# A two-layer decoder trunk on one core: half of the attention's key blocks on GpSimd in place of a third, roots by way of PSUM, head norms ahead in the queues

## The chip, the core and the metric

One core of a Trainium2 chip runs the whole program. The metric is device time in microseconds, the median of three runs. TensorE is PE here, VectorE DVE, ScalarE ACT, GpSimd POOL, and SyncE, which issues the DMAs, SP.

## What is computed

Two layers over 2048 positions of width 1024, in float32. Layer 0 is gated linear attention (GLA), layer 1 forgetting attention (FoX) with 16 heads of 64. After each mixer a per-layer embedding is added (PLE: a projection times the sigmoid of a gate). A norm ends it. The part that the change touches most:

```python
def fox_mixer(h, w_in, b_f, q_gain, k_gain, w_out):
    q, k, v, g, f_logit = jnp.split(h @ w_in, ...)
    log_f = jax.nn.log_sigmoid(f_logit + b_f)
    qh = rms_norm(to_heads(q, FOX_HEADS), q_gain)   # the head norms
    kh = rms_norm(to_heads(k, FOX_HEADS), k_gain)
    o = fox_attention(qh, kh, vh, log_f)            # softmax(q k^T / 8 + c[t] - c[s], causal) v
    return (o * jax.nn.silu(g)) @ w_out
```

## The kernel before

Positions are cut into four chunks of 512 columns (c = 0 to 3); a tile is 128 partitions by 512 columns, one PSUM bank. Every float32 operand of a large matmul is split into a high part, rounded to the matmul's type, and a low part, the rest; a product is three matmuls (high by high, high by low, low by high). Names end in h and l for the parts: xnh, xnl the normed input, ogh, ogl the gated mixer output, wh, wl weights, kh, kl temporaries.

Streams (Python generators: dense work, attention, maxima, norms, gates) emit operations to a planner, `Streams` (L72), which simulates the engines with its own costs and decides the order of every engine; the program is then written in that order and each engine runs its queue strictly in it. Operations that are ready on an engine go by level and then by age (`able`, L206 to L210); a lower level goes first. All instructions bear the line of the planner's call, so they are told apart by tile names.

In layer 1, `attention` (L1331) takes heads in order. For a head and chunk it goes over nk = 4(c+1) key blocks of 128 keys. For a block PE computes the scores pS (As with B, Es with Dc) into a PSUM bank; ACT makes exp into Ph (rounded) and a second, full exp; the difference is Pl; PE adds V by Ph and V by Pl to the output po two blocks later (LAG). Blocks whose number is a multiple of G_OF put the full exp into SBUF (P0, accg or Pf: names P, ag, Pf in the trace) and let POOL take the difference and the running sum accg (ag). The other blocks put it back into the bank and let DVE take the difference (Pl<-bank) and the sum (acc<-bank). At the end of a head POOL adds accg to acc. `maxima` (L1269) computes the scores' maxima one head ahead: a matmul (Dm with Es) per 128 queries into a bank, a DVE maximum (mx), and at the end of the head m4c, a transpose on PE and a row of Es. At most M_LIVE of these matmuls are under way.

`qk_unit` (L1212) projects a pair of heads and norms them: a square on ACT, high part kh on ACT and low part kl on POOL, a sum over the head by a matmul with onesb, `rsqrt` (L620), y, and the parts again. `rsqrt` is Ln, Exp and Square on ACT and two DVE instructions: q = (pin + eps) q, and out = (q - 1.5) y, both into SBUF (names rs). `join` (L1414) does the denominators of a head pair in the same manner.

`out1` (L1500) is the output projection of a chunk, `ple1` (L1507) its PLE, `finish` (L1492) the last norm: eight instructions hr<-hr,gcol,rs on DVE, each followed by a store. A chunk's attention output that comes before the PLE of the chunk ahead is stored in DRAM (os) and reloaded by way of hx, in two buffers, when that PLE is done.

Of the kernel before, what the change touches and what calls it, by code (L numbers as in the profile page):

```python
# [16 lines left out]
ALU = mybir.AluOpType  # L17
# [9 lines left out]
EPS = 1e-6  # L27
GH, DK, DV = 4, 128, 256
FH, HD = 16, 64
# [4 lines left out]
PARTS = ("xnh", "xnl", "ogh", "ogl", "hr")  # L34


BANKS, K_D, K_V, K_M, M_LIVE = 8, 0, 0, 1, 3

PB, PF, PL, LAG = 3, 2, 3, 2

# [9 lines left out]

V_KS, N_O, N_G = ((0,), (1,), (2, 3), (4, 5), (6, 7)), 5, 2

G_OF = 3

Q_W, Q_C, Q_M = -1, 1, 1
P_A, P_M, P_D = 2.5, 0.5, 3

POOL_F = 3
# [13 lines left out]
class Streams:  # L72
# [19 lines left out]
    def spawn(self, gen, prio):  # L92
        self.count += 1
        self.streams.append([prio, self.count, gen, self.now])

    def mark(self, key):
        self.marks[key] = self.now
# [109 lines left out]
    def at(self, *aps):  # L207

        return self.over([self.hist[k][0] for x in aps for k in self.parts(x) if k in self.hist and self.hist[k][0]])
# [38 lines left out]
    def bank(self, keep=0):  # L248

        return lambda: sorted(self.over(q)() for q, i in self.banks)[keep] if len(self.banks) > keep else INF  # L250
# [6 lines left out]
    def give(self, ap):  # L257
        self.banks.append((self.users(ap), self.bankno[ap.tensor.name]))
# [53 lines left out]
def trunk_kernel(ctx: ExitStack, tc: tile.TileContext, a: dict, out: bass.AP, layers: int = 2):  # L312
# [4 lines left out]
    nc = SimpleNamespace(vector=Engine(nc0.vector, sq_, "V"), scalar=Engine(nc0.scalar, sq_, "A"), gpsimd=Engine(nc0.gpsimd, sq_, "G"), sync=Engine(nc0.sync, sq_, "H"))  # L317
# [29 lines left out]
    @contextmanager  # L347
    def level(n):

        sq_.level += n  # L350
        try:
            yield
        finally:
            sq_.level -= n
# [4 lines left out]
    def psa(name):  # L359
        return banks[sq_.take()]  # L360
# [4 lines left out]
    def parted(src, square, eng):  # L365

        hl = [tmp.tile([P, T], F32R, tag="k" + x, name="k" + x, bufs=KB) for x in "hl"]
        if square:
            q = t2("q", "sq", 2)
            nc.scalar.activation(q, src, AF.Square)  # L370
            src = q
        split(*hl, src, eng)
        return hl

    def total(name, w, src, square, eng):

        yield tmp.able("kh", KB)
        hl = parted(src, square, eng)
        names = {x.tensor.name for x in hl}
        tmp.held |= names  # L380
        yield at(*hl)
        yield bank()
        pn = psa(name)
        for n in range(2):
            mm(pn, w, hl[n], start=(n == 0), stop=(n == 1))
        tmp.held -= names
        return pn

    def t2(name, tag, bufs):
        return tmp.tile([P, T], F32, tag=tag, name=name, bufs=bufs)  # L390

    def mm(dst, w, x, start=True, stop=True):
        n = dst.free_size()
        sq_.op("P", [dst], [w, x], max(n, 64) * (4 if x.dtype == F32 or n < 256 else 1) / 2400.0 + 0.0134, partial(nc0.tensor.matmul, dst, w, x, start=start, stop=stop))
# [4 lines left out]
    def rdma(dst, src):  # L399
        nc.sync.dma_start(dst.bitcast(F32), src.bitcast(F32))  # L400


    def split(hi, lo, src, eng):
        nc.scalar.copy(hi, src)
        eng.tensor_tensor(lo, src, hi.bitcast(F32), ALU.subtract)
# [172 lines left out]
    def steps(pairs, dst, n0, total):  # L578

        for n, (w, x) in enumerate(pairs):  # L580
            yield at(w, x)
            mm(dst, w, x, start=(n0 + n == 0), stop=(n0 + n == total - 1))
# [8 lines left out]
    def unit(name, x, nm):  # L591

        yield bank(K_D)
        dst = psa(name)
        for i in range(2):
            yield from half(dst, x, nm, i)
        return dst
# [22 lines left out]
    def rsqrt(pin, scale, out=None):  # L620
        yq = tmp.tile([P, 2, T], F32, tag="rs", name="rs", bufs=2)
        n = pin.free_size()
        y, q = yq[:, 0, 0:n], yq[:, 1, 0:n]
        nc.scalar.activation(y, pin, AF.Ln, bias=epsb, scale=scale)
        nc.scalar.activation(y, y, AF.Exp, scale=-0.5)
        nc.scalar.activation(q, y, AF.Square, scale=(0.5 * scale) ** 0.5)
        nc.vector.scalar_tensor_tensor(q, pin, EPS / scale, q, ALU.add, ALU.mult)
        q2 = q if out is None else out
        nc.vector.scalar_tensor_tensor(q2, q, 1.5, y, ALU.subtract, ALU.mult)
        return q2  # L630

    def sigmoid(z, tag, bufs):
# [8 lines left out]
    class SumSq:  # L641
# [36 lines left out]
        def root(self, out=None):  # L678
            pn = yield from total("nq_p", onesr, self.acc, False, nc.vector)
            r = rsqrt(pn, 1.0 / D, out)  # L680
            give(pn)
            return r
# [177 lines left out]
    L = {}  # L860
# [351 lines left out]
    def qk_unit(c, u, col):  # L1212

        pq = yield from unit("pqk", xn, "wqk")

        def rest():
            if col == 0 or u:

                yield ("sum", c, 2 * u - col)
            pn = yield from total("qk_n", L["onesb"], pq, True, nc.gpsimd)  # L1220
            mark(("sum", c, 2 * u + 1 - col))
            yield tmp.able("kh", KB)
            r = rsqrt(pn, 1.0 / HD)
            give(pn)
            y = t2("qk_y", "ny", 2)
            nc.vector.scalar_tensor_tensor(y, pq, L["qkg"][:, col : col + 1], r, ALU.mult, ALU.mult)
            give(pq)
            nm = "qk"[col]
            hi = tmp.tile([P, T], F32R, tag="kh", name=nm + "h", bufs=KB)
            lo = tmp.tile([P, T], F32R, tag="kl", name=nm + "l", bufs=KB)  # L1230
            split(hi, lo, y, nc.gpsimd)
            for j in range(2):
                js = slice(j * HD, (j + 1) * HD)
                d = L["KS"][c][2 * u + j] if col else L["QS"][2 * u + j][c]
                rdma(d[64:128], (hi if col else lo)[js])
                rdma(d[0:64], (lo if col else hi)[js])
            mark(("qk"[col], c, u))

        spawn(rest(), 0)
# [91 lines left out]
    def attention():  # L1331
        nxt = None
        for i in range(NCH * FH):
# [11 lines left out]
            for kb in range(nk):  # L1345
# [21 lines left out]

                if kb % G_OF == 0:
                    if kb == 0:
                        Pf = P0 = L["f"].tile([P, T], F32, tag="P0", name="P0", bufs=2)  # L1370
                    elif kb == G_OF:
                        Pf = accg = L["f"].tile([P, T], F32, tag="ag", name="ag", bufs=2)
# [6 lines left out]
                    nc.gpsimd.tensor_tensor(Pl[:, c0:], Pf[:, c0:], Ph[:, c0:].bitcast(F32), ALU.subtract)  # L1379
                    if kb > G_OF:  # L1380
                        with level(Q_C):
# [32 lines left out]
    def join(c, h, po, acc):  # L1414

        i, u = h % 2, h // 2
        if i == 0:
            pair["o"] = L["f"].tile([P, T], F32, tag="op", name="op", bufs=1)
        op = pair["o"]
        own, oth = slice(i * 64, i * 64 + 64), slice(64 - i * 64, 128 - i * 64)  # L1420
        hb = t2("hb", "sq", 2)
        nc.scalar.copy(hb[own], po[oth])
        nc.vector.tensor_tensor(op[own], hb[own], po[own], ALU.add)
        give(po)
        pair[i] = acc
        if i == 0:
            return
        a0, a1 = pair[0], pair[1]

        def rest():  # L1430
            yield at(a0, a1)
            yield ("sg1", c, u)
            yield bank()
            pd = psa("den")
            mm(pd, L["onesh"][:, 0], a0, stop=False)
            mm(pd, L["onesh"][:, 1], a1, start=False)
            yq = tmp.tile([P, 2, T], F32, tag="rs", name="dn", bufs=2)
            y, q = yq[:, 0], yq[:, 1]
            nc.scalar.activation(y, pd, AF.Ln)
            nc.scalar.activation(y, y, AF.Exp, scale=-1.0)  # L1440
            nc.vector.tensor_tensor(q, pd, y, ALU.mult)
            give(pd)
            nc.vector.scalar_tensor_tensor(q, q, 2.0, y, ALU.subtract, ALU.mult)
            nc.vector.scalar_tensor_tensor(q, op, -1.0, q, ALU.mult, ALU.mult)
            nc.gpsimd.tensor_tensor(q, q, sgs[c, u], ALU.mult)
            if c and ("ple1", c - 1) not in sq_.marks:

                nc.sync.dma_start(os[c][:, u], q)
                later.append((c, u))
            else:  # L1450
                split(og[0][:, u], og[1][:, u], q, nc.gpsimd)
            mark(("den", c, u))
            mark(("og1", c, u))

        spawn(rest(), 0)

    sgs, later = {}, []
# [153 lines left out]
```

## Time and profile before

| what | value |
|---|---|
| median of three runs | 3096.41 us (3092.79 to 3096.66) |
| the profiled execution | 3096.0 us, its span 3094.3 us |
| PE, busy share | 97% |
| DVE, ACT, POOL, busy share | 72%, 62%, 37% |
| granted TensorE clock, mean | 0.987 |
| on the chain that ended last | PE 86%, DVE 6%, DMA 3%, ACT 2% |

Layer 0 takes about the first 1100 us. A busy PE counts also matmuls at half clock, so the number of matmuls in a stretch says more than the share. An engine's idle time is put down to what ended it.

### The profile page before, as it was taken

To read this page: it belongs to the slowest core of one execution; us is meant where nothing else is said; L and a number is where in the kernel's file an instruction comes from. 1 tells how busy PE (TensorE), PEld (TensorE's weight loads), DVE (VectorE), ACT (ScalarE), POOL (GpSimd) and SP (SyncE) were. 2 spreads that over 40 slices of the span, in tenths; PEclk is the share of its full clock that TensorE was granted. 3 is DMA by queue.
4 is the path that set the end of the run, shared out by engine and by line. 5 is a ranking of instruction groups with operands and counts; after the bars stand their busy time and mean duration, and the time that the engine had idled before them with its cause. 6 is when DMAs were issued, how large, how long until landed. Compare 5 with 4: busy or idle time off the path is not lost.

```text
span 3094.3 us, 43470 instructions
## 1 busy us (share of the span) xinstructions
PE 3000.7 (97%) x13568; PEld 2418.8 (78%) x13568; DVE 2225.9 (72%) x3979; ACT 1905.0 (62%) x3651; POOL 1136.0 (37%) x941
## 2 busy tenths in 40 slices
PE   8989999999999999999999999999999999999887
PEld 6878887888788878777788776888777878778666
DVE  7686767667765765675766768775888788888835
ACT  6565665657565465664656656565757677667635
POOL 1232222213222234453433424343545455455531
PEclk9999999999999999999999999999999999999989
DMA  5565667556632567987768776778677677666654
GB/s 192 183 209 177 204 201 234 187 195 214 218 109 82 178 189 246 279 266 249 228 215 273 234 224 204 228 213 263 215 241 228 216 243 227 208 190 193 209 175 140
DMA packets 379737, 648.15 MB, mean 209 GB/s; under 512 B 43097, under 2 KB 78433, under 8 KB 379506
## 3 DMA queue, kind: packets, MB, share of 16 engines
q1 hardware_dynamic: 379506, 645.37, 65.6%
q8 instruction: 108, 1.77, 0.2%
q14 instruction: 123, 1.01, 0.1%
HBM read 521.86 MB, written 123.21 MB: 208 GB/s over the span
## 4 chain that ended last, share of the span: by engine, by line
PE 86%; DVE 6%; DMA 3%; ACT 2%; issue 1%; POOL 1%; SPq 1%; DVEq 0%; ACTq 0%; POOLq 0%
PE bank L176 86%; DVE ny L176 1%; DMA B<-KS 1%; DVE rs L176 1%; DMA Dm<-KS 1%; DVE mx L176 1%; DMA hx<-hs 1%; SPq L176 1%; ACT rs L176 1%; DVE hr L176 1%; DVE Pl L176 0%; DVE acc L176 0%; ACT Ph L176 0%; DVE wl L176 0%; DVE ogl L176 0%
## 5 line engine op out<-in xcount | busy, mean ns | idle before, releaser
L176 ACT ACTIVATE Ph<-bank 128x512 fp32r<-128x512 f32 (+2 forms) x640 | 335.9, 545 | 95.1 <-PE bank L176 45.1
L176 DVE TENSOR_TENSOR wl<-wr,wh 128x512 fp32r<-128x512 f32 x332 | 264.6, 804 | 158.2 <-ACT wh L176 126.9
L176 PE MATMUL bank<-xnh,wh 128*128 128x512 f32 x1128 | 323.8, 397 | 0.8 <-ACT Ph L176 0.6
L176 PE MATMUL bank<-xnl,wh 128*128 128x512 f32 x1128 | 322.6, 394 | 0.0
L176 PE MATMUL bank<-xnh,wl 128*128 128x512 f32 x1128 | 322.3, 393 | 0.0
L176 DVE TENSOR_TENSOR Pl<-bank,Ph 128x512 fp32r<-128x512 f32 (+2 forms) x400 | 245.9, 615 | 74.0 <-ACT bank L176 72.3
L176 DVE TENSOR_REDUCE mx<-bank 128x1 f32<-128x512 f32 x384 | 249.2, 682 | 54.9 <-PE bank L176 53.8
L176 PE MATMUL bank<-ogh,wh 128*128 128x512 f32 x912 | 260.6, 397 | 15.9 <-ACT ogh L176 15.9
L176 ACT CAST wh<-wr 128x512 fp32r<-128x512 f32 x332 | 203.0, 615 | 113.7 <-PE bank L176 57.5
L176 PE MATMUL bank<-ogl,wh 128*128 128x512 f32 x912 | 258.4, 395 | 1.0 <-DVE ogl L176 0.9
L176 PE MATMUL bank<-ogh,wl 128*128 128x512 f32 x912 | 255.8, 393 | 0.0
L176 PE MATMUL bank<-As,B 128*128 128x512 f32 (+2 forms) x640 | 242.6, 379 | 7.2 <-DMA B<-KS 3.2
L176 PEld LDWEIGHTS bank<-xnh,wh 128*128 128x128 f32 x1128 | 211.2, 189 | 47.7 <-ACT Ph L176 1.5
L176 PE MATMUL bank<-Pl,V 128*128 128x512 f32 (+2 forms) x640 | 238.3, 372 | 9.6 <-POOL Pl L176 5.8
L176 PEld LDWEIGHTS bank<-xnl,wh 128*128 128x128 f32 x1128 | 210.2, 189 | 42.7 <-issue 0.2
L176 PEld LDWEIGHTS bank<-xnh,wl 128*128 128x128 f32 x1128 | 209.5, 188 | 42.8 <-issue 0.6
L176 PE MATMUL bank<-Ph,V 128*128 128x512 f32 (+2 forms) x640 | 238.4, 372 | 0.1
L176 PE MATMUL bank<-Es,Dc 128*128 128x512 f32 (+2 forms) x640 | 236.4, 369 | 1.6 <-DMA Es<-mr 1.6
L176 PE MATMUL bank<-Dm,Es 128*128 128x512 f32 (+2 forms) x640 | 223.4, 376 | 10.8 <-DVE acc L176 7.6
L176 ACT ACTIVATE bank<-bank 128x512 f32<-128x512 f32 (+2 forms) x400 | 219.2, 548 | 0.0
L176 PEld LDWEIGHTS bank<-ogh,wh 128*128 128x128 f32 x912 | 171.7, 190 | 54.5 <-ACT ogh L176 19.1
L176 POOL TENSOR_TENSOR ag<-ag,Pf 128x512 f32<-128x512 f32 (+1 forms) x112 | 125.2, 1118 | 211.9 <-ACT Pf L176 172.1
(271 smaller groups left out, 7077.2 us busy)
## 6 DMA issues: line engine op xcount, KB each, us to landing
B<-KS SPq DMA_DIRECT2D x160, 256.0 KB
V<-VS SPq DMA_DIRECT2D x160, 256.0 KB
Dm<-KS SPq DMA_DIRECT2D x160, 132.0 KB
Dc<-KS SPq DMA_DIRECT2D x160, 132.0 KB
wr<-gla_wv SPq DMA_DIRECT2D x64, 256.0 KB
wr<-gla_wqk SPq DMA_DIRECT2D x64, 256.0 KB
wr<-gla_wg SPq DMA_DIRECT2D x64, 256.0 KB
wr<-gla_wo SPq DMA_DIRECT2D x64, 256.0 KB
```

The source lines that it names most:

```text
L176: q.emit()
```

## The change

Five constants and places change. G_OF goes from 3 to 2, so POOL takes every second key block. M_LIVE goes from 3 to 2. The first DVE instruction of `rsqrt` and of the denominators writes its result into the PSUM bank that it reads, and the second reads it there, so that neither reads two SBUF tensors. A level Q_N = -1 is put on the square, parts, root and y of the head norms.

```diff
-BANKS, K_D, K_V, K_M, M_LIVE = 8, 0, 0, 1, 3
+BANKS, K_D, K_V, K_M, M_LIVE = 8, 0, 0, 1, 2
...
-G_OF = 3
+G_OF = 2
...
+Q_N = -1
...
-    def total(name, w, src, square, eng):
+    def total(name, w, src, square, eng, lv=0):
 
         yield tmp.able("kh", KB)
-        hl = parted(src, square, eng)
+        with level(lv):
+            hl = parted(src, square, eng)
...
         nc.scalar.activation(q, y, AF.Square, scale=(0.5 * scale) ** 0.5)
-        nc.vector.scalar_tensor_tensor(q, pin, EPS / scale, q, ALU.add, ALU.mult)
+
+        nc.vector.scalar_tensor_tensor(pin, pin, EPS / scale, q, ALU.add, ALU.mult)
         q2 = q if out is None else out
-        nc.vector.scalar_tensor_tensor(q2, q, 1.5, y, ALU.subtract, ALU.mult)
+        nc.vector.scalar_tensor_tensor(q2, pin, 1.5, y, ALU.subtract, ALU.mult)
...
-            pn = yield from total("qk_n", L["onesb"], pq, True, nc.gpsimd)
+            pn = yield from total("qk_n", L["onesb"], pq, True, nc.gpsimd, Q_N)
             mark(("sum", c, 2 * u + 1 - col))
             yield tmp.able("kh", KB)
-            r = rsqrt(pn, 1.0 / HD)
+            with level(Q_N):
+                r = rsqrt(pn, 1.0 / HD)
+                y = t2("qk_y", "ny", 2)
+                nc.vector.scalar_tensor_tensor(y, pq, L["qkg"][:, col : col + 1], r, ALU.mult, ALU.mult)
             give(pn)
-            y = t2("qk_y", "ny", 2)
-            nc.vector.scalar_tensor_tensor(y, pq, L["qkg"][:, col : col + 1], r, ALU.mult, ALU.mult)
             give(pq)
...
-            nc.vector.tensor_tensor(q, pd, y, ALU.mult)
+            nc.vector.tensor_tensor(pd, pd, y, ALU.mult)
+            nc.vector.scalar_tensor_tensor(q, pd, 2.0, y, ALU.subtract, ALU.mult)
             give(pd)
-            nc.vector.scalar_tensor_tensor(q, q, 2.0, y, ALU.subtract, ALU.mult)
```

The planner then orders every engine anew. Each engine's instructions are the same in number but for those named in the prediction; three places are shown.

DVE at the end of attention, before: the last norm of chunk 2 (hr), with the blocks of the head before the last (Pl, acc) and the maxima of the last head (mx, printed as ISA) around it.

```order
L176 SCALAR_TENSOR_TENSOR rs_192<-rs_192 128x512
L176 TENSOR_TENSOR Pl_8138<-bank_90,Ph_8137 128x384
L176 SCALAR_TENSOR_TENSOR hr<-hr,gcol,rs_192 128x512 x8
L176 TENSOR_TENSOR acc_8153<-bank_90,acc_8153 128x384
L176 TENSOR_TENSOR bank_92<-bank_92,limT 128x128
```

And now, the same eight instructions; op is the output of the last head pair, kl the split of the norm's sum.

```order
L178 TENSOR_TENSOR op_8150<-sq_184,bank_93 64x512
L178 SCALAR_TENSOR_TENSOR ny_166<-bank_89,ny_166 128x512
L178 TENSOR_TENSOR ny_166<-ny_166,bank_88 128x512
L178 TENSOR_TENSOR nacc_235<-nacc_235,sq_185 128x512
L178 TENSOR_TENSOR kl_201<-nacc_235,kh_200 128x512
...
L178 SCALAR_TENSOR_TENSOR bank_90<-bank_90,rs_162 128x512
L178 SCALAR_TENSOR_TENSOR rs_162<-bank_90,rs_162 128x512
L178 SCALAR_TENSOR_TENSOR hr<-hr,gcol,rs_162 128x512 x8
L178 TENSOR_TENSOR pl_228<-rs_192,ph_227 128x512 x2
```

Before, an acc and all that follows of the last head come behind the eight; now the last head's last op comes ahead of them.

PE in the last head, before, from the transpose of its maxima (ident) on:

```order
L176 MATMUL bank_92<-ident,m4c_8155 4x128
L176 MATMUL bank_93<-As_8043,B_8134 128x512
L176 MATMUL bank_93<-Es_8046,Dc_8051 128x512
L176 MATMUL bank_87<-Ph_8140,V_8152 128x256
L176 MATMUL bank_87<-Pl_8141,V_8152 128x256
L176 MATMUL bank_89<-As_8043,B_8134 128x512
L176 MATMUL bank_89<-Es_8046,Dc_8051 128x512
L176 MATMUL bank_87<-Ph_8142,V_8152 128x256
L176 MATMUL bank_87<-Pl_8143,V_8152 128x256
```

And now, a few blocks into the last head:

```order
L178 MATMUL bank_89<-As_8043,B_8134 128x512
L178 MATMUL bank_89<-Es_8046,Dc_8051 128x512
L178 MATMUL bank_87<-ogh,wh_102 128x512 x2
L178 MATMUL bank_87<-ogl,wh_102 128x512 x4
L178 MATMUL bank_87<-ogh,wl_103 128x512 x3
L178 MATMUL bank_93<-Ph_8137,V_8135 128x512
L178 MATMUL bank_93<-Pl_8138,V_8135 128x512
L178 MATMUL bank_90<-As_8043,B_8134 128x512
L178 MATMUL bank_90<-Es_8046,Dc_8051 128x512
```

Before, scores and values follow each other with nothing between; now matmuls of ple1(2) (ogh, ogl) stand between the blocks.

PE between the last of ple1(2) (ph, pl by weights) and out1(3) (ogh by wh_96) in the new order; xnh, xnl is the last gate, onesh a denominator, onesr the sum of the norm.

```order
L178 MATMUL bank_88<-ph_227,wl_101 128x512 x2
L178 MATMUL bank_92<-xnh,wh_102 128x512 x4
...
L178 MATMUL bank_92<-xnh,wxl_8035 128x512 x4
L178 MATMUL bank_91<-acc_8153,onesh 128x512
L178 MATMUL bank_91<-acc_8136,onesh 128x512
L178 MATMUL bank_90<-kh_200,onesr 128x512
L178 MATMUL bank_90<-kl_201,onesr 128x512
L178 MATMUL bank_94<-ogh,wh_96 128x512 x4
L178 MATMUL bank_94<-ogl,wh_96 128x512 x4
```

Before, ple1(2) is done ahead of the last head's blocks; now only these matmuls lie between it and out1(3).

## Rows read from the trace of the kernel before

**Rows 1.** The page, part 1: busy time, share of the span, instructions.
```profile
PE 3000.7 (97%) x13568; PEld 2418.8 (78%) x13568; DVE 2225.9 (72%) x3979; ACT 1905.0 (62%) x3651; POOL 1136.0 (37%) x941
```
**Rows 2.** Windows: length, then PE, PEld, DVE, ACT, POOL busy (count); clock, DMA share, GB/s.
```profile
2300.00:2920.00 620.00, 609.00 (x2686) 486.02 (x2685) 519.39 (x992) 420.02 (x837) 310.46 (x251) 0.99 0.70 216
2920.00:2980.00 60.00, 38.23 (x145) 28.16 (x144) 41.14 (x69) 34.52 (x69) 31.22 (x25) 0.80 0.43 141
```
**Rows 3.** PE's waits, 1230 to 2980, and the last of 2920 to 2980: us, times, longest.
```profile
PE bank L176 <- DVE acc L176: 18.5, 5, 7.6
PE bank L176 <- DVE m4c L176: 6.2, 1, 6.2
PE bank L176 <- POOL Pl L176: 5.8, 5, 1.7
...
PE bank L176 <- DVE acc L176: 7.6, 1, 7.6
```
**Rows 4.** Windows of 20 us, columns as in rows 2.
```profile
2900.00:2920.00 20.00, 19.97 (x84) 14.97 (x83) 16.91 (x27) 15.05 (x28) 10.45 (x8) 1.00 0.74 231
1500.00:1520.00 20.00, 16.94 (x66) 13.29 (x67) 16.77 (x26) 11.43 (x22) 13.41 (x10) 0.91 0.40 112
1880.00:1900.00 20.00, 15.03 (x54) 9.60 (x53) 18.00 (x38) 15.10 (x31) 12.02 (x10) 0.89 0.55 158
2740.00:2760.00 20.00, 12.87 (x44) 9.66 (x43) 19.08 (x26) 11.86 (x23) 9.58 (x7) 0.74 0.29 82
2720.00:2740.00 20.00, 20.00 (x91) 16.46 (x90) 19.96 (x28) 15.90 (x31) 11.91 (x9) 1.00 0.68 210
```
**Rows 5.** DVE's timeline at the end of attention: start, length, instruction.
```profile
2930.15 8.96 DVE L176 SCALAR_TENSOR_TENSOR hr<-hr,gcol,rs 128x512 f32<-128x512 f32 x8
2939.03 0.55 DVE L176 TENSOR_TENSOR acc<-bank,acc 128x384 f32<-128x384 f32 x1
```
**Rows 6.** PE's timeline there; in brackets the wait before it and for whom.
```profile
2908.90 0.40 PE L176 MATMUL bank<-Dm,Es 128*128 128x512 f32 x1
...
2939.63 0.80 PE L176 MATMUL bank<-Dm,Es 128*128 128x512 f32 x1 [7.60 <-DVE acc L176]
2946.61 0.37 PE L176 MATMUL bank<-ident,m4c 128*4 128x128 f32 x1 [6.18 <-DVE m4c L176]
...
2970.03 0.50 PE L176 MATMUL bank<-Pl,V 128*128 128x512 f32 x1 [1.68 <-POOL Pl L176]
```
**Rows 7.** Groups by form, 2300 to 2920 (the two of rs: whole span): busy, mean ns.
```profile
L176 DVE TENSOR_TENSOR Pl<-bank,Ph 128x512 fp32r<-128x512 f32 x142 | 97.1, 684 | 23.8 <-ACT bank L176 23.0
...
L176 POOL TENSOR_TENSOR Pl<-Pf,Ph 128x512 fp32r<-128x512 f32 x47 | 62.7, 1334 | 0.0
L176 POOL TENSOR_TENSOR ag<-ag,Pf 128x512 f32<-128x512 f32 x47 | 62.1, 1322 | 90.5 <-ACT Pf L176 81.7 <-PE bank L176 8.6
...
L176 DVE SCALAR_TENSOR_TENSOR rs<-rs 128x512 f32<-128x512 f32 x128 | 103.6, 811 | 1.6
L176 DVE SCALAR_TENSOR_TENSOR rs<-bank,rs 128x512 f32<-128x512 f32 x99 | 68.0, 687 | 81.0 <-ACT rs L176 80.8
```
**Rows 8.** Window of tile Pl on POOL alone: length, busy (count); clock, DMA.
```profile
2300.00:2920.00 620.00, 129.98 (x103) 0.99 0.70 216
```
**Rows 9.** Tile rs on DVE, whole span: count, ns min/median/max.
```profile
L176 DVE SCALAR_TENSOR_TENSOR rs<-rs x130: 426/686/1793, 22.6 to 3086.4; 128x512 f32<-128x512 f32 x128, 128x256 f32<-128x256 f32 x2
L176 DVE SCALAR_TENSOR_TENSOR rs<-bank,rs x101: 410/691/694, 21.4 to 3086.0; 128x512 f32<-128x512 f32 x99, 128x256 f32<-128x256 f32 x2
```
**Rows 10.** The chain, 2600 on (start, us, what), and tile hx, 1400 on.
```profile
2916.69 4.12 DMA hx<-os
...
L176 ACT CAST ogh<-hx x9: 602/618/632, 1619.9 to 2941.6; 128x512 fp32r<-128x512 f32 x9
L176 POOL TENSOR_TENSOR ogl<-hx,ogh x9: 1261/1292/1737, 1620.6 to 2942.3; 128x512 fp32r<-128x512 f32 x9
```

## The prediction

> **What bounds the kernel now.** I began with the page's busy shares [rows 1]: PE is busy 97% of the span, DVE 72%, ACT 62%, POOL 37%. No work is taken off PE, so a gain can only come from time in which PE stands still or runs at a low clock. Next the stretches of the second layer [rows 2]: from 2300 to 2920 us PE is busy 609 of 620 us, but DVE too 519 of 620 (84%), POOL 310 (50%). From 2920 to 2980 PE is busy only 38 of 60 us, at a granted clock of 0.80. Then PE's waits [rows 3]: of the 18.5 us in which PE waited for DVE's acc, 7.6 are one wait after 2920, and 6.2 for the last m4c follow it. POOL is waited for 5.8 us, in the same 60 us: the row reads alike for the whole second layer and for the stretch. [...] An undisturbed slice holds 91 matmuls; 2740 to 2760 holds 44, 1880 to 1900 54, 1500 to 1520 66. In all three DVE is 84 to 95% busy: **PE waits where DVE's queue is late.**
>
> What DVE's queue held in the worst place is in [rows 5]: eight `hr` instructions of finish(2) take 8.96 us in a row, and the acc that frees a bank, and the maxima behind it, come after them. PE stands for 7.60 and 6.18 us [rows 6]. In the same 60 us, with hardly any dense matmul left to put between, PE waits for POOL in five key blocks, 5.8/5 = 1.16 us on average [rows 3] and 1.68 in the last of them [rows 6].
>
> **The change part by part.** *Key blocks.* The instruction counts of the new program give 80 fewer 512-wide Pl and acc on DVE, 16 fewer 256-wide, 16 more 384-wide; on POOL the reverse. An acc works over the same columns as its Pl, and I price it by the Pl's row. By [rows 7] DVE loses 80 x 2 x 0.684 = 109 us and gains, for 16 x 128 columns more, 16 x 2 x 0.684/4 = 5 us: 104 us less. POOL gains 80 x (1.334 + 1.322) = 212 us and loses 16 x 2.66/4 = 11 us: 201 us more. ACT still makes two exponentials a block. In 2300 to 2920 POOL made 103 Pl [rows 8]; at 8 blocks of a head's 16 in place of 6 that is a third more, some 34: DVE falls by 34 x 1.36 = 46 us to 76%, POOL rises by 34 x 2.66 = 90 us to 65%. Neither is then the bound of that stretch. DVE instructions with two SBUF inputs may get slower as POOL is busier (next part); I leave that in the range.
>
> *Roots.* 131 instructions of 512 columns (99 roots, 32 denominators), which read two SBUF tensors, read one from PSUM instead. By the mean of rs<-rs and rs<-bank (0.811 and 0.687 us [rows 7]), 131 x 0.124 = 16 us of DVE. The medians are 686 and 691 ns and the longest 1793 and 694 [rows 9]: what goes is the long ones. Bounds: 0 and 16 us. It is DVE time, nearly all beside PE, so no term of its own.
> [...]
>
> *Head norms first, two maxima in flight.* Neither adds an instruction. Level -1 moves the squares, kl, roots and y of a head norm ahead in ACT's, DVE's and POOL's order; behind them queue Pl and acc, each later by one or two instructions of 0.7 us (1.3 on POOL). Two maxima in flight still allow one in about (0.40 + 0.68)/2 = 0.54 us [rows 6, 7], while PE needs 5 matmuls a key block, 5 x 0.22 = 1.1 us. I take 0 for both, between -5 and +5 us: what they do is to spread the maxima.
>
> *Order.* The order of every engine changes, PE's total does not. Two places decide. At the end of attention the eight `hr` now stand behind the last acc, and matmuls of ple1(2) stand between the last head's blocks, where before there was attention alone. At the rate of 2900 to 2920 (84 matmuls in 20 us) the 145 of 2920 to 2980 need 34.5 us: **25.5 us are lost there.** What returns in another form: ple1(2) now ends just ahead of out1(3), so the stored og of chunk 3 is reloaded late, by way of two hx buffers. A round is a transfer of 4.1, a cast of 0.62 and a split of 1.29 us [rows 10]; k = 2 and 3 come with the second round, cast at about 6.0 + 4.1 + 1.2 = 11.3 us and split by 13.9, while PE has before it 24 gate matmuls, two denominators and the sum, some 8 us. It will wait 4 to 6 us, and some matmuls may follow at half clock: I keep 9 of the 25.5 us, a gain of 16 (bounds 0 and 25).
>
> The three slices inside lost (91 - 44)/91 x 20 = 10.3, 8.1 and 5.5 us: 24 us. Bursts of `ny` and `hr` remain, on a queue with 8 points more room. I take half, 12 us (bounds 0 and 24). New waits on POOL's Pl: of the 103 blocks of 2300 to 2920 not one held PE, all five waits fall in the 60 us after them [rows 3, 8]; now dense matmuls stand there. I take four waits, +4 us. GLA's stalls I leave as they are; its order moves too, by a few us either way.
>
> **Sum:** 3096.0 (the profiled execution; 3094.3 of span and 1.7 around it; the median is 3096.4) - 16 - 12 + 4 = **3072 us**.
>
> **The rivals.** (a) *DVE's room empties its queue*: nearly all of the 25 and 24 us return, 3096 - 25 - 24 + 3 = 3050. For it: every large wait of the second layer is behind DVE. Against it: the bursts of eight stay, and the reload is new.
> (b) *The stalls only move*: a plan made anew has its own late places, and the reload and POOL eat the gain: 3096. That the program does not do what it says is excluded by its order; that the order alone decides is this case.
> (c) *POOL becomes what PE waits for*, slower. A POOL block's Pl takes 1.33 us against DVE's 0.68, behind the same two exponentials, and with every second block on POOL the ag of one stands right before the Pl of the next. Where PE has no dense matmul between a block's scores and its values, it pays 1.16 us (the mean of the five waits). The point is the number: beyond (24 + 4)/1.16 = 24 such blocks of 320 the gain is gone; at one in eight, 40 blocks, it is 46 us in place of the 4: 3072 + 42 = 3114. Against it: the 103 blocks without a wait at 50% POOL, 65% to come.
> [...]
>
> **How the numbers follow.** Forecast 0.50 (its own range 3060 to 3085), (a) 0.20, (b) 0.12, (c) 0.18. About 0.2%, 6 us, is what a measurement of this kernel can tell from no change. Faster: 0.50 + 0.20 = 0.70; same: 0.12; slower: 0.18. The range reaches from just under (a), 3045, to just over (c), 3115; it leaves out perhaps 0.07 below and 0.09 above.
>
> **What would show it.** Right: DVE near 2120 us busy, POOL near 1340; no wait of PE on acc or m4c over 3 us at the end of attention; some 4 to 6 us of PE waiting for ACT's or POOL's og at the start of out1(3); rs<-bank near 0.69 us. The slice counts inside say how much of the 12 us came. Wrong: PE waiting on POOL Pl for over 25 us in all, or new half-clock stretches in 1230 to 2900 of the length of the old ones.

## The result, and the profile after

The changed kernel takes **3059.4 us** (median, 3053.3 to 3062.0), the kernel before, run beside it, 3095.2: a ratio of 0.988, 95% interval 0.9865 to 0.9900, some 36 us faster. The forecast was 3072 in a range of 3045 to 3115.

The page's first part and windows of the changed kernel, columns as in [rows 1, 2, 4]:

```profile
PE 2992.0 (98%) x13568; PEld 2417.1 (79%) x13568; DVE 2145.0 (70%) x3819; ACT 1906.8 (62%) x3651; POOL 1332.8 (44%) x1101
```
```profile
2300.00:2920.00 620.00, 614.21 (x2733) 493.41 (x2733) 486.01 (x924) 425.67 (x851) 415.46 (x337) 1.00 0.70 215
2920.00:2980.00 60.00, 56.48 (x230) 44.63 (x229) 24.85 (x28) 17.31 (x30) 15.81 (x12) 0.94 0.79 268
1500.00:1520.00 20.00, 12.21 (x37) 8.90 (x36) 16.40 (x30) 11.71 (x24) 13.14 (x10) 0.66 0.21 62
1880.00:1900.00 20.00, 20.00 (x88) 15.82 (x87) 13.79 (x27) 9.90 (x18) 8.21 (x7) 1.00 0.74 229
2740.00:2760.00 20.00, 19.88 (x87) 15.39 (x85) 18.91 (x28) 16.88 (x34) 14.18 (x12) 1.00 0.68 214
2980.00:3000.00 20.00, 11.80 (x39) 7.97 (x38) 10.54 (x14) 9.65 (x17) 4.02 (x4) 0.73 0.27 88
```

POOL does 197 us more, DVE only 81 less. Of the three poor slices [rows 4], 1880 and 2740 are whole again (88 and 87 matmuls for 54 and 44), 1500 is worse (37 for 66, at a granted clock of 0.66). The 60 us after 2920 hold 230 matmuls for 145, but the next 20 us only 39 of some 90, at a granted clock of 0.73. PE's waits from 1230 to 2980 (us, times, longest), the head of the list:

```profile
PE bank L178 <- DVE rs L178: 6.0, 1, 6.0
PE bank L178 <- ACT ogh L178: 2.6, 2, 1.7
PE bank L178 <- DVE Pl L178: 2.3, 3, 1.2
PE bank L178 <- ACT Pf L178: 2.2, 2, 1.3
PE bank L178 <- POOL Pl L178: 2.0, 2, 1.8
```

The 18.5 us for acc and 6.2 for m4c of [rows 3] are gone, and so are most of the waits for POOL. Laid over each other by work done (each matmul weighed by its usual spacing), the two traces part as follows: first layer -9 us at 484 and +9 in small steps around it, 0 in all; 1150: -2; 1500: +6.6; 1750 to 1860: -8; 1880: -13; 2300: +3; 2740: -9; from 2900 on: -22 until 2980, then 10 of them lost again at 2988.

That last loss is the final norm of ple1(3). The changed kernel's PE there, with its waits in brackets:

```profile
2987.87 0.51 PE L178 MATMUL bank<-kl,onesr 128*128 128x512 f32 x1 [0.22 <-DVE kl L178]
2993.37 1.46 PE L178 MATMUL bank<-ogh,wh 128*128 128x512 f32 x2 [5.00 <-ACT ogh L178]
2996.59 1.46 PE L178 MATMUL bank<-ogh,wh 128*128 128x512 f32 x2 [1.76 <-ACT ogh L178]
```

### The profile page after: what moved, and what is told of

Same layout as the page of the kernel before. It is cut to its first block, busy times and chain, and to the rows that moved or that the text cites. A ratio compares the mean times of both kernels' runs of the same rounds, so it can differ in the third digit from the quotient of the medians.

```text
span 3060.3 us, 43654 instructions
## 1 busy us (share of the span) xinstructions
PE 2992.0 (98%) x13568; PEld 2417.1 (79%) x13568; DVE 2145.0 (70%) x3819; ACT 1906.8 (62%) x3651; POOL 1332.8 (44%) x1101
## 4 chain that ended last, share of the span: by engine, by line
PE 89%; DVE 3%; ACT 3%; DMA 2%; issue 1%; POOL 1%; SPq 0%; DVEq 0%; ACTq 0%; POOLq 0%
PE bank L178 89%; ACT rs L178 1%; DMA B<-KS 1%; DVE ny L178 1%; SPq L178 0%; DVE wl L178 0%; DVE hr L178 0%; DVE bank L178 0%; DMA hr<-hs 0%; DMA Dm<-KS 0%; ACT wh L178 0%; DMA hr<-xT 0%; ACT Ph L178 0%; ACT sg L178 0%; DVE rs L178 0%
## 5 line engine op out<-in xcount | busy, mean ns | idle before, releaser
L178 DVE TENSOR_TENSOR Pl<-bank,Ph 128x512 fp32r<-128x512 f32 (+1 forms) x320 | 194.3, 607 | 107.0 <-ACT bank L178 98.3
L178 POOL TENSOR_TENSOR ag<-ag,Pf 128x512 f32<-128x512 f32 x192 | 226.5, 1180 | 78.3 <-ACT Pf L178 54.1
L178 PE MATMUL bank<-Dm,Es 128*128 128x512 f32 (+2 forms) x640 | 230.6, 377 | 3.5 <-DMA Dm<-KS 1.7
L178 POOL TENSOR_TENSOR Pl<-Pf,Ph 128x512 fp32r<-128x512 f32 x192 | 228.5, 1196 | 2.1 <-ACT Ph L178 1.7
```

Of the source, the lines that this page charges most:

```text
L178: q.emit()
```

## The experiments

Every edit makes the planner write all orders anew, so "undo one part" also draws a new order. Hence three kinds of runs: parts undone or done alone; the order kept while an instruction or a place changes; and the work kept while the order is drawn anew. Each ratio is to the kernel before, run beside it: 3095.2 us beside the changed kernel, 3092.6 to 3093.0 beside the others. "Layer 2" is the profiled span less the start of the first copy carry<-rs (the first forget gate), "last As" the start of the last score matmul on tile As: how long attention lasts. Both are read from one profiled execution.

| kernel | blocks on GpSimd | roots | us (range) | ratio, 95% interval | layer 2 | last As |
|---|---|---|---|---|---|---|
| before | every 3rd | SBUF | 3092.6 | 1 | 1984.7 | 2970.4 |
| changed | every 2nd | PSUM | 3059.4 (3053.3-3062.0) | 0.988 [0.9865, 0.9900] | 1950.8 | 2911.3 |
| u_gof3 | every 3rd | PSUM | 3124.4 (3121.9-3126.6) | 1.010 [1.0086, 1.0117] | 2010.4 | 2996.6 |
| u_roots | every 2nd | SBUF | 3092.7 (3089.0-3098.2) | 1.000 [0.9992, 1.0009] | 1981.1 | 2955.7 |
| u_mlive3 | every 2nd | PSUM | 3063.8 (3062.0-3065.0) | 0.990 [0.9890, 0.9917] | 1951.1 | 2915.3 |
| u_qn0 | every 2nd | PSUM | 3068.5 (3067.6-3071.6) | 0.992 [0.9907, 0.9934] | 1962.3 | 2921.0 |
| o_gof2 | every 2nd | SBUF | 3070.7 (3067.5-3072.5) | 0.993 [0.9914, 0.9939] | 1956.9 | 2914.6 |
| o_roots | every 3rd | PSUM | 3099.2 (3096.4-3105.6) | 1.003 [1.0016, 1.0035] | 1993.2 | 2978.3 |
| p_gof2_roots | every 2nd | PSUM | 3089.0 (3086.3-3091.8) | 0.999 [0.9980, 0.9998] | 1974.1 | 2925.7 |
| f_roots_sbuf | every 2nd | SBUF | 3071.3 (3068.2-3072.5) | 0.993 [0.9915, 0.9940] | 1958.7 | 2920.0 |
| t_hr_late | every 3rd | SBUF | 3093.4 (3086.1-3097.3) | 1.000 [0.9992, 1.0010] | 1984.6 | 2970.4 |
| t_ple_late | every 3rd | SBUF | 3105.0 (3098.9-3108.7) | 1.004 [1.0024, 1.0049] | 1985.6 | 2949.0 |
| s_before | every 3rd | SBUF | 3079.2 (3078.7-3084.3) | 0.996 [0.9947, 0.9972] | 1987.7 | 2958.2 |
| s_after | every 2nd | PSUM | 3057.4 (3057.1-3061.5) | 0.989 [0.9873, 0.9904] | 1956.9 | 2891.7 |

### One part undone

```diff
u_gof3:   -G_OF = 2
          +G_OF = 3
u_mlive3: -BANKS, K_D, K_V, K_M, M_LIVE = 8, 0, 0, 1, 2
          +BANKS, K_D, K_V, K_M, M_LIVE = 8, 0, 0, 1, 3
u_qn0:    -Q_N = -1
          +Q_N = 0
u_roots:  the three hunks of the change in rsqrt and join taken back
```
u_gof3: 

> The changed kernel with every third key block on GpSimd again (the other three edits stay). Theory (DVE's room): DVE busy rises by about 80 us to 2225, POOL falls to 1135, and the gain of the second layer (some 34 us of the 36) goes: 3085 to 3100 us, with waits of PE for DVE of several us each in 1800 to 3000. Rival (the plan alone): the order is made anew and its late places fall anywhere; 3050 to 3075, with the second layer no worse than in the changed kernel.

u_mlive3: 

> The changed kernel with three maxima in flight again. Theory: nothing beyond what a new order does, 3054 to 3066 us. Rival (two in flight spread DVE's bursts): slower by 10 us or more, 3070 and up, with new waits of PE for DVE's maxima or acc.

u_roots: 

> The changed kernel with the roots and denominators through SBUF again. Theory: DVE is busy some 10 to 16 us more, the time moves by what the order does: 3054 to 3072 us; the wait of 6.0 us at 1502 us, for a bank that the second root instruction now holds, goes or shrinks, and the first layer's stall at 483 us (10 us with its half clock) may come back, as its order changes with the roots. Rival (the roots carry the gain): 3075 and up.

u_qn0: 

> The changed kernel with the head norms' work at the level of the rest. Theory: the order is made anew, 3054 to 3070 us. Rival (the head norms' place carries a part of the gain): slower by 10 us or more, with waits of PE for kh, kl or q and k of the next heads in 1230 to 2900.

With every third key block again the kernel is 65 us slower than the changed one and 31 slower than before, more than any case expected. Without the roots all of the gain is gone, as the rival had it. The other two cost 4 and 9 us, less than the rivals asked. PE's waits of u_gof3 from 1230 to 3000 and, behind the dots, of 2940 to 3000:

```profile
PE bank L178 <- DVE m4c L178: 18.8, 4, 15.2
PE bank L178 <- POOL Pl L178: 11.1, 10, 1.7
PE bank L178 <- DMA Dm<-KS: 7.6, 10, 3.6
...
PE bank L178 <- DVE m4c L178: 15.2, 1, 15.2
```
Attention ends at 2997 there, 85 us later than in the changed kernel, and the last heads' maxima hold PE as before. PE waits for POOL 11.1 us, over five times the changed kernel's 2.0, with POOL busy 1135 us in place of 1333.

### Parts alone

```diff
o_gof2:        -G_OF = 3
               +G_OF = 2
o_roots:       the three hunks of the roots put into the kernel before
p_gof2_roots:  both
```
o_gof2: 

> The kernel before with every second key block on GpSimd alone. Theory as predicted (DVE's room is the gain): 3065 to 3080 us. Rival (without the roots the room does not pay, as undoing the roots showed): 3085 to 3105 us, with waits of PE of over 5 us at the end of attention again.

p_gof2_roots: 

> The kernel before with two of the four edits: every second key block on GpSimd, roots through PSUM. Theory (these two carry the gain, undoing either lost it all; the other two are worth 4 and 9 us at most): 3059 to 3075 us. Rival (the gain hangs on the one order that all four make): 3085 us and up.

o_roots: 

> The kernel before with the roots and denominators by way of PSUM alone. Theory (the instruction is worth DVE time also without GpSimd's new blocks, 16 us, and the first layer's stall at 484 us goes with its new order, 8 us): 3080 to 3090, attention still ends last, with PE idle there. Rival (the plan made anew eats it): 3090 and up.

The key blocks alone gain 22 us, as predicted for DVE's room; the roots alone lose 7, and both together give 4: in these two the rival's figure came, not the theory's. So the parts don't add up as times. Layer 2 sorts them: all eight kernels with every second block on GpSimd lie at 1951 to 1981 us (mean 1961.5), all six with every third at 1985 to 2010 (mean 1991.0). The 30 us between the means are the finding; the gap of 3.5 us between the nearest two is less than executions of one kernel differ by (3088 to 3097 for the kernel before), and f_roots_sbuf and t_hr_late share their orders with the changed kernel and the kernel before. Three pairs that differ in this edit alone (changed and u_gof3, o_gof2 and before, p_gof2_roots and o_roots) give 60, 28 and 19 us. The roots, in pairs of new orders, give 30 for (u_roots), 17 against (p_gof2_roots and o_gof2) and 8.5 against (o_roots): no sign of their own that way.

How fast attention goes shows in tile As on PE (us busy, count; clock, DMA share, GB/s) from 2500 to 2900. Before:

```profile
2500.00:2700.00 200.00, 37.52 (x98) 1.00 0.75 230
2700.00:2900.00 200.00, 35.82 (x92) 0.97 0.61 190
```
The changed kernel:

```profile
2500.00:2700.00 200.00, 41.10 (x107) 0.99 0.73 225
2700.00:2900.00 200.00, 40.97 (x108) 1.00 0.63 197
```
u_gof3:

```profile
2500.00:2700.00 200.00, 38.90 (x101) 0.97 0.71 214
2700.00:2900.00 200.00, 35.44 (x92) 0.94 0.56 174
```
215 blocks against 190 and 193. o_gof2 has 214. This is not the whole of it: o_roots has 204 and u_roots 195.

The key blocks' move does two things at once. It takes work off DVE, and it frees PSUM banks sooner: a block on GpSimd gives its bank back behind ACT's second exponential, a block on DVE only behind acc. From its score matmul on, a bank is held 3.8 us by a DVE block and 2.1 us by a GpSimd block in the kernel before, 3.5 and 2.2 in the changed one (medians). No run parts the two.

### The order kept: what the roots' instruction is worth

```diff
+    def as_planned(op, plan, real):
+
+        getattr(nc.vector, op)(*plan)
+        sq_.todo[-1].emit = partial(getattr(nc0.vector, op), *real)
...
-        nc.vector.scalar_tensor_tensor(pin, pin, EPS / scale, q, ALU.add, ALU.mult)
...
+        as_planned("scalar_tensor_tensor", (pin, pin, EPS / scale, q, ALU.add, ALU.mult), (q, pin, EPS / scale, q, ALU.add, ALU.mult))
```
and likewise for the second result and the denominators: the planner sees the bank, the chip gets SBUF.

> The changed kernel with every engine's order kept, instruction for instruction, and only the 163 root and denominator results put into SBUF again in place of the bank. Undoing the roots with a new order gave 3093 us. Theory (the roots act through the order that the planner makes of them): 3057 to 3068 us, DVE busy some 16 us more, the end of attention as in the changed kernel. Rival (the instruction itself carries the gain, by its time on a loaded DVE): 3080 us and up.

The results put back are 133 (101 roots and 32 denominators), not 163. 3071.3 for 3059.4: **12 us** are the instruction's, at one and the same order (8.6 between the two profiled spans); between theory and rival. DVE is busy 2173.6 us for 2145.0, 28.6 more where 16 were expected. Groups of f_roots_sbuf and of the changed kernel by form (busy, mean ns):

```profile
L178 DVE SCALAR_TENSOR_TENSOR rs<-rs 128x512 f32<-128x512 f32 x128 | 113.0, 883 | 1.7
```
```profile
L178 DVE SCALAR_TENSOR_TENSOR rs<-bank,rs 128x512 f32<-128x512 f32 x128 | 87.8, 686 | 1.7
```
The old form's mean rose from 811 ns [rows 7] to 883 with GpSimd's new blocks. It has two SBUF inputs. Of its 132 in f_roots_sbuf (the 4 small ones of the forget gates among them) the 66 with no POOL instruction in their time have a median of 686 and a longest of 694 ns; the 66 with one have a mean of 1074 and a longest of 1784. Pl<-bank,Ph of 512 columns, which reads a bank, takes at most 694 in the changed kernel and before, with a POOL instruction in its time (169 of 192, 171 of 272) or without.

### The order kept: what PE waits for at the end of attention

t_hr_late, on the kernel before:
```diff
-            nc.vector.scalar_tensor_tensor(hr[:, k], hr[:, k], gcol[:, G_FIN, k : k + 1], r, ALU.mult, ALU.mult)
-            nc.sync.dma_start(out[c][:, k], hr[:, k])
+            with level(2 if c == NCH - 2 else 0):
+                nc.vector.scalar_tensor_tensor(hr[:, k], hr[:, k], gcol[:, G_FIN, k : k + 1], r, ALU.mult, ALU.mult)
+                nc.sync.dma_start(out[c][:, k], hr[:, k])
```


> The kernel before, whose order stays the same up to the end of attention, with the eight hr of finish(2) put behind acc and the maxima in DVE's queue. Theory (the burst is what PE waits for there): the waits of 7.60 and 6.18 us shrink below 3 us each, 8 to 16 us are gained: 3078 to 3086 us. Rival (attention is alone at that place, with no dense matmul left, and its own chain of maximum, exponential, Pl and values sets the pace): at most 4 us gained, 3089 to 3096, the waits turn into waits for ACT, Pl or Es.

Nothing gained: the rival's size. PE's waits of 2920 to 2980 in t_hr_late:

```profile
PE bank L176 <- DVE m4c L176: 8.3, 1, 8.3
PE bank L176 <- POOL Pl L176: 5.8, 5, 1.7
PE bank L176 <- DMA Es<-mr: 4.3, 1, 4.3
```
The wait for acc is gone, those for m4c and for Es have grown: m4c's matmul starts at 2943.9 in place of 2946.6, the scores behind it at 2949.1 in both. The row of Es that these scores need comes by DMA. Its issue and the matmul that waits for it, before:

```profile
2947.31 0.63 SPq L176 DMA_DIRECT2D Es<-mr  x1
2949.11 0.76 PE L176 MATMUL bank<-Es,Dc 128*128 128x512 f32 x1 [1.64 <-DMA Es<-mr]
```
and in t_hr_late, with the part of the burst that now comes behind m4c:

```profile
2943.75 5.33 DVE L176 SCALAR_TENSOR_TENSOR hr<-hr,gcol,rs 128x512 f32<-128x512 f32 x5
2944.50 0.36 SPq L176 DMA_DIRECT2D B<-KS  x1
2944.96 0.63 SPq L176 DMA_DIRECT2D Es<-mr  x1
2949.05 0.80 PE L176 MATMUL bank<-Es,Dc 128*128 128x512 f32 x1 [4.30 <-DMA Es<-mr]
```
From issue to matmul it takes 4.1 us in place of 1.8, right behind the load of B, which before came after it. So the 2.7 us won at m4c were lost here, and three of the eight `hr` still stand ahead of m4c. The run shows that moving most of the burst brings m4c forward by 2.7 us and not by the 13.8 us of the two waits; whether a quick Es would have kept the 2.7 was not tried.

What PE lacks there too is other work. Weight matmuls on tile wh (us busy, count; clock, DMA share, GB/s), before:

```profile
2920.00:2940.00 20.00, 0.39 (x1) 0.83 0.64 207
2940.00:2960.00 20.00, 0.00 (x0) 0.66 0.49 162
```
and in the changed kernel, where attention has ended and ple1(2) and out1(3) follow:

```profile
2920.00:2940.00 20.00, 9.02 (x27) 0.83 0.58 189
2940.00:2960.00 20.00, 10.79 (x46) 1.00 0.92 324
```
t_ple_late gives the kernel before such work there, with the loads of DVE and POOL as they were:
```diff
-G_LAG, OUT_AT, PLE_AT = 3, ((1, 2), (2, 3), (3, 7)), ((1, 3), (2, 3), (3, 9))
+G_LAG, OUT_AT, PLE_AT = 3, ((1, 2), (2, 3), (3, 7)), ((1, 3), (2, 3), (3, 11))
```


> The kernel before, with ple1(2) two places later in the list of dense work of chunk 3; the orders stay the same up to the last 130 us or so, and DVE's and POOL's loads stay as they are. In its order 61 weight matmuls stand between the maximum and the scores of the last head, where the kernel before has none; but a head further ahead is left without any. Theory A (the loss at the end of attention is that no weight matmul is left for PE while the last heads' chain runs; whoever has them there keeps the time): 10 to 20 us gained, 3073 to 3083. Theory B (DVE's load sets how fast attention goes, so the hole only moves to the head further ahead): within 5 us of the kernel before, 3088 to 3098.

Theory B, and worse: 12 us slower. PE's order parts from the old one earlier than written, near 2790 us, and the hole moved there, to 2780 to 2840. Tile wh in that stretch, before:

```profile
2780.00:2800.00 20.00, 7.16 (x24) 1.00 0.61 190
2800.00:2820.00 20.00, 4.24 (x16) 1.00 0.73 230
2820.00:2840.00 20.00, 7.84 (x28) 1.00 0.58 191
```
and in t_ple_late:

```profile
2780.00:2800.00 20.00, 0.95 (x4) 0.79 0.52 150
2800.00:2820.00 20.00, 0.00 (x0) 0.95 0.48 146
2820.00:2840.00 20.00, 0.00 (x0) 0.83 0.34 107
```
The profiled execution took 3098.9 us, the fastest of the six, so the trace and the layer 2 of the table show only a part of the 12 us.

### The work kept: what an order is worth

```diff
-    AFTER = {"P": 0.2, "A": 0.15, "V": 0.15, "G": 0.12, "H": 2.2}
+    AFTER = {"P": 0.2, "A": 0.15, "V": 0.16, "G": 0.12, "H": 2.2}
```
s_before: 

> The kernel before with one number of the planner changed that no instruction depends on: the delay it assumes behind a DVE instruction, 0.16 for 0.15 us. The work is the same, every order is made anew. If orders of the same work lie close together (differences of 10 us between the kernels of this study then belong to the edits): 3086 to 3100 us. If the order alone is worth what the edits seemed to be: outside of that, by up to 20 us on either side.

s_after: 

> The changed kernel with the same number of the planner changed. If orders of the same work lie close together: 3053 to 3067 us. If the order alone decides: 3070 to 3095, most likely with attention last or with waits of 4 to 7 us at other norms.

s_before is 13 us faster than before, with the same work, and so outside the range for orders that lie close together. Its layer 2 is as long as before (1987.7 for 1984.7); all of the gain is in the first layer, where a stall at 200 us is gone. That window before, and in s_before:

```profile
200.00:220.00 20.00, 11.69 (x35) 8.22 (x34) 18.09 (x22) 8.11 (x14) 7.74 (x5) 0.74 0.60 208
```
```profile
200.00:220.00 20.00, 19.66 (x86) 15.70 (x85) 19.68 (x27) 12.43 (x22) 8.07 (x6) 1.00 0.77 245
```
s_after loses the stall too, but gets one at 472 (7.1 us) and a layer 2 that is 6 us longer: 3057.4, the same as the changed kernel within their ranges. So two orders of the same work lie up to 13 us apart here, and a difference of that size between single kernels can't be put down to an edit. These are two redraws; the scatter of orders may be wider.

## Why the prediction was right, and where not

**The sum.** -24 was forecast, -36 came: right in sign and within the range, 0.6 us outside the likeliest case's own 3060 to 3085, on the side of rival (a). That it came so near is in part the draw of the order: p_gof2_roots, with both edits that take time off DVE, came to 3089.

**DVE's room is the gain: shown for the edit, in part for the reason.** That the key blocks' move carries the gain is shown by layer 2 of the eight kernels with every second block on GpSimd against the six without, and o_gof2 alone has -22 us. That DVE time costs time is shown at one and the same order by f_roots_sbuf (28.6 us of DVE, 12 us). How much of the key blocks' gain is DVE's time and how much the sooner freed banks is open. The sign that the prediction read, DVE at 84 to 95% in the three poor slices, was weak: the undisturbed slice of [rows 4], 2720 to 2740, has DVE busy for 19.96 of its 20 us.

**"104 us less" on DVE, and 16 of the roots: mis-sized.** 120 were priced (the sign "DVE near 2120" counts the 104 alone; 2145 came), 81 came; o_gof2 alone shows 55 (2225.9 to 2170.8) where 104 stood. The durations were as priced (Pl and acc lose 104 us of them). But neighbours in a full queue overlap; they start 0.60 us apart at 0.67 each, as here in t_hr_late:

```profile
2927.21 0.68 DVE L176 TENSOR_TENSOR Pl<-bank,Ph 128x512 fp32r<-128x512 f32 x1
2927.81 0.67 DVE L176 TENSOR_TENSOR acc<-bank,acc 128x512 f32<-128x512 f32 x1
2928.41 0.67 DVE L176 TENSOR_REDUCE mx<-bank 128x1 f32<-128x512 f32 x1
```
And in o_gof2 the instructions with two SBUF inputs got slower by some 30 us in all as POOL was busier (rs<-rs 12 of them): the effect that the prediction left "in the range". POOL's 201 were 197.

**The roots "no term of its own": wrong.** Priced as 16 us of DVE beside PE; with POOL's new blocks they are 28.6 us of DVE, and 12 us of time at the same order. The two edits belong together: the first makes two SBUF inputs dearer (rs<-rs 811 ns before, 904 in o_gof2), the second takes 131 of them away.

**The end of attention: the size was right, the reason was not borne out.** -16 and +4 were forecast, -12 came. "The eight `hr` now stand behind the last acc" was named as one of two things that return the time; t_hr_late moved most of them and gained nothing. The other, matmuls of ple1(2) between the last blocks, is what t_ple_late gave the kernel before, and that was no gain without the room. What fits the runs is which ends last: attention, whose chain leaves PE idle, or the weight matmuls, which wait for no such chain. With less in DVE's queue attention is done at 2911 in place of 2970, and weight matmuls are left. No run changes this alone.

**What is late next: right that something is, wrong what.** og's reload costs 2.6 us, not 4 to 6. The residual's reload hr<-hs is late instead: its last piece is issued at 2975.5, DVE's add comes at 2980.1, and the norm's chain then has no matmul beside it, some 10 us with the low clock (granted 0.50 from 2990 to 3002). u_mlive3 and s_after, in which attention ends at 2915 and 2892 us, have this wait of 5.0 us too; t_ple_late has one of 6.2 us for kh near it. Whether the queue on SP makes the piece late was not tried.

**The slices inside: "I take half, 12 us".** Of the 20 us windows of [rows 4], 1880 and 2740 came back nearly whole, 22 us with the stretches beside them; 1500 got 6.6 worse; and 8 us between 1750 and 1860 were in no row of the prediction (1780 to 1860 held 319 matmuls before, 353 now). The slice at 1500, at a granted clock of 0.66 (0.50 from 1506 to 1518), comes nearest to the prediction's own sign of being wrong (new half-clock stretches as long as the old ones; before, 0.50 was granted from 2746 to 2754, where 512-wide matmuls start 0.43 us apart, for 0.23 after 2756 at 1.00). There PE waits 5.96 us for a bank that now is held until the second root result. f_roots_sbuf, which frees it one result earlier at the same order, waits 3.60 there and 2.39 for Ph a little later: the hold costs 2.4 us, and the next wait takes it back.

**POOL becomes the bound, rival (c): fell.** 2.0 us in two waits, for four at 1.16 forecast. Nor do these waits follow POOL's load: o_roots, with POOL at 1132 us, has

```profile
PE bank L176 <- POOL Pl L176: 13.2, 15, 1.7
```
and 2 wh matmuls between 2740 and 2780. They come mostly where no weight matmul stands beside attention, as in [rows 3]: 13 of these 15 have none among the twelve matmuls ahead of them.

**The first layer "as it is": right in sum only.** 9 us won at 484, 9 lost in small pieces. The stall at 484 is in all kernels that were planned with SBUF roots except s_before (a smaller one at 474), and in none with PSUM roots except s_after; f_roots_sbuf has SBUF roots at the changed order and lacks it. So there the order acts, not the instruction.

**Head norms and two maxima "0, between -5 and +5": open.** Undoing them costs 9 and 4 us, and p_gof2_roots, without both, is 30 us behind the changed kernel. One order each, against a scatter of 13 us in two redraws, can't tell an effect from a draw. Several orders for each would; they weren't tried.

## What to carry to other kernels

Where an engine is full of independent work and shares it with a dependent chain, look at which of the two ends last: here room for the chain's engine went with the gain at the end, and moving a burst out of its queue, or holding independent work back, paid nothing. Where a planner draws the order, measure first how far two orders of the same work lie apart (up to 13 us here), compare edits as groups of orders, and price an instruction by keeping the order fixed. When work goes to GpSimd, count DVE's instructions with two SBUF inputs (here the mean of rs<-rs rose from 811 to 904 ns in o_gof2), and let them read a bank where one is at hand (686 ns for rs<-bank,rs in the changed kernel, 12 us at one and the same order).

## What the hardware showed beyond what was expected

In f_roots_sbuf rs<-rs, with two SBUF inputs of 512 columns, takes 686 ns (median) with no POOL instruction in its time and up to 1784 with one; rs<-bank,rs, which reads a bank and writes SBUF, takes at most 695 there. In the changed kernel writing into the bank costs little: bank<-bank,rs has a mean of 698 ns, rs<-bank,rs 686. Successive DVE instructions of 0.67 us start 0.60 us apart (t_hr_late, from 2927.81 us), so that a removed one gives back less than its duration: in o_gof2 DVE's durations fall by 74 us in sum, its busy time by 55.
